# The last projection of a decoder block as Strassen's seven block products, its weight sums made on GpSimd during the attention

## The chip, the cores and the metric

One core of one Trainium2 chip runs the whole program. The metric is the device time of one execution in microseconds (us), the median of the runs shown. One more execution was profiled; every row below is from it.

## The reference, cut to what matters

One layer of a decoder block with 1024 positions and a model width of 1024, in float32. Two places of it matter here: the stick-breaking attention (eight heads), during which the change lets GpSimd work, and the last product, with w_down (2816 x 1024), which the change rearranges.

```python
def _stick_breaking(q, k, v):
    for nb in range(T // QBLK):
        ...
        z = jnp.einsum('bhqd,bhkd->bhqk', qb, kb).astype(jnp.float32) * scale
        log_rest = jnp.where(mask, jax.nn.log_sigmoid(-z), 0.0)
        after = lax.cumsum(log_rest, axis=3, reverse=True) - log_rest
        a = jnp.where(mask, jnp.exp(jax.nn.log_sigmoid(z) + after), 0.0)
        outs.append(jnp.einsum('bhqk,bhkd->bhqd', a.astype(vb.dtype), vb))
...
        up = u @ w_up[layer]
        up = lax.conv_general_dilated(up, ...) + conv_b[layer]
        gate, val = up[..., :D_FF], up[..., D_FF:]
        h = h + (jax.nn.silu(gate) * val) @ w_down[layer]
    return _rms_norm(h, final_norm_w)
```

## The kernel before, in words

The program goes through input projections, the stick-breaking attention, the sparse attention, the output projection, the up product (`up`) and the down product (`down`). Nearly all float32 products are made as three matmuls: each operand is split into a high half (a copy by ScalarE, L193) and a low half (the rest, a subtraction, L194), and high x high, high x low and low x high are added up in PSUM. The up product is already done by Strassen's scheme in Winograd's form, with the names P1 to P7 (L1454 to L1456).

**The stick-breaking attention** (`sb_attend`). The work is cut into 48 pieces, each of two query blocks with up to four key blocks. `sb_front` makes the logits of a query block on TensorE (L425, L426, L428), two sigmoids on ScalarE (L429, L430), a running product on VectorE (the scan, L436), and the product of the two on GpSimd (L439, tile `A`, 96 of them; L441 clears the part above the diagonal). `sb_turn` transposes the finished `A` on TensorE (L455), two pieces later (`SB_LAG = 2`), and `sb_back` multiplies it with the values (L475). Between them a second generator, `fill`, is advanced: the projections of the next head pair, whose weights are loaded on SyncE's queue (`wr`, L204) and split by ScalarE and GpSimd (`wl`, L194). Each engine and SyncE's queue runs its instructions strictly in an order fixed when the program is built; the builder places an instruction where its inputs are expected to be ready, so that an engine's order need not be the order of the source.

**The down product** (`down`). The 2816 rows of w_down are 22 row blocks of 128, the 1024 positions two chunks of 512. For each chunk `c`, each of the 22 row blocks and each of four position blocks and two column halves, three matmuls of 512 columns run (`mms`, L1588 to L1590): 2 x 22 x 8 x 3 = 1056. In a chunk the eight PSUM banks hold the eight sums. `load_w` loads a row block of the weights once and splits it (ScalarE and GpSimd, tiles `dh`, `dl`; the first eight have their place in `qn` and `mts`, which the up product has left); `load_act` loads the activations `act_d`, which the up product has written to DRAM, and splits them on ScalarE and VectorE (`ah`, `al`). At each chunk's start and end four row blocks are taken together (`GROUP`), so that rows of the output end one after another; their residual is added (L1624), the squares are summed, and `finish` scales and stores them.

Of the kernel before, what the change touches and what calls it, by code (L numbers as in the profile page):

```python
# [10 lines left out]
F32 = mybir.dt.float32  # L11
F32R = mybir.dt.float32r
# [68 lines left out]
class Kern:  # L81
# [479 lines left out]
                    nc.vector.memset(self.score[rows, i, cur + 1:16], NEG)  # L561


    def compress_in(self, kv, wp, vp):

        nc, a = self.nc, self.a
        w = self.load_cols(wp, a["w_in"], (C_KC, C_VC)[kv], bufs=3, rbufs=2, parts=2)
        for c in range(2):
            pm = self.ps("mm")
            yield from self.mm3_steps(pm, [w[k] + self.u(k, c) for k in range(KT)])  # L570
            src = self.tl(vp, [P, 512], "vt")
            nc.scalar.activation(src, pm, AF.Copy)
            nc.sync.dma_start(self.kct_d[kv][:, c * 512:c * 512 + 512], src)
            yield
# [493 lines left out]
    def run(self):  # L1068
# [15 lines left out]
        with self.pool("sbv", "right") as vp:  # L1084
            st_b, st_a = ExitStack(), ExitStack()
            stk = [None, st_b.enter_context(self.pool("stkb", "right"))]
            stk[0] = st_a.enter_context(self.pool("stka", "right"))
            ops = []
            with self.pool("xin") as xin:
                proj = self.sb_project(0, wp, stk[0], vp, ops, xin)  # L1090
                self.load_norm(xin, vp, mxs, proj, stk[1])
                for _ in proj:
                    pass
            with self.pool("sbw") as work:
                fill, due = iter(()), 0.0
                got = [ops, [], [], []]

                def start(p):
                    nonlocal fill
                    for _ in fill:  # L1100
                        pass
                    if p < 3:
                        fill = self.sb_project(p + 1, wp, stk[1 - p % 2], vp, got[p + 1])
                    else:
                        st_a.close()
                        fill = self.compress_keys(st_a.enter_context(self.pool("cin", "right")), wp, vp)
                    self.pace = PACE[p == 3]
                    return got[p]

                for _ in self.sb_attend(start, work, mxs):  # L1110
                    due += self.pace
                    while due >= 1.0:
                        due -= 1.0
                        next(fill, None)
                for _ in fill:
                    pass
            st_a.close()
            st_b.close()
# [148 lines left out]
    def mlp(self, mxs):  # L1267
# [125 lines left out]
        for _ in fill:  # L1393
            pass
        st_r.close()
        self.weights, self.acts = {}, {}
        self.up(p1)
        self.down(st_up)

# [58 lines left out]
    def up(self, p1):  # L1458
# [3 lines left out]
        for i in range(NF):  # L1462
# [34 lines left out]
            if last:  # L1497
                for _ in range(AHEAD):
                    self.prepare()
                self.load_w(0)  # L1500
                self.load_w(1)
            bb = self.ps(tags[1])
            self.product(bb, i, "P6", True)
            u2 = self.scratch()
# [3 lines left out]
            u3 = self.scratch()  # L1508
            nc.vector.tensor_add(u3, bc, u2)
            if last:  # L1510
                for j in range(GROUP):
                    if j > 1:
                        self.load_w(j)
                    self.load_act(j, 0)
            bd = self.ps(tags[3])
            self.product(bd, i, "P5", True)

# [14 lines left out]
            gate(1)  # L1532


    def load_w(self, i):

        homes = ((self.qn, 0), (self.qn, 4), (self.mts, 4), (self.mts, 0))
        if i < 2 * len(homes):
            if i in self.weights:
                return  # L1540
            t, lo = homes[i // 2]
            v = t[:, lo:lo + 4].rearrange("p a b t -> p (a b t)")[:, 2048 * (i % 2):2048 * (i % 2) + 2048]
            dh, dl = v[:, 0:T], v[:, T:2048]
        else:
            dh, dl = (self.tl(self.dp, [P, T], t, 5, F32R) for t in ("dh", "dl"))
        raw = self.tl(self.rawp, [P, KT, P], "wr", 4).rearrange("p k c -> p (k c)")
        self.nc.sync.dma_start(raw, self.a["w_down"][i * P:(i + 1) * P, :])
        self.split_w(raw, dh, dl)
        self.weights[i] = (dh, dl)

    def load_act(self, i, c):

        if c == 0 and i < GROUP:
            raw = self.scratch()
            ah, al = (t[:, i, :] for t in self.R["P7"])
        else:
            raw = self.tl(self.dp, [P, 512], "ar", 3)
            ah, al = (self.tl(self.dp, [P, 512], t, 7, F32R) for t in ("ah", "al"))
        self.nc.sync.dma_start(raw, self.act_d[i][:, c * 512:c * 512 + 512])
        self.split_w(raw, ah, al, self.nc.vector)  # L1560
        self.acts[i, c] = (ah, al)

    def down(self, st_up):
        nc, a = self.nc, self.a
        weights, acts = self.weights, self.acts
        rows = []

        def finish(tb, y, ss):
            r = self.rstd(ss, 1, 1.0 / DM, True)
            nc.scalar.activation(y[:, 0:512], y[:, 0:512], AF.Copy, scale=r[:, 0:1])  # L1570
            nc.vector.scalar_tensor_tensor(y[:, 512:DM], hs[tb][:, 512:DM], r[:, 0:1], self.fnw[:, 512:DM],
                                           op0=ALU.mult, op1=ALU.mult)
            for i in range(2):
                nc.sync.dma_start(a["out"][tb * P:(tb + 1) * P, i * 512:i * 512 + 512], y[:, i * 512:i * 512 + 512])

        hs = {}
        with ExitStack() as st_2:
            for c in range(2):
                banks = {}

                def mms(i, tb, hf):
                    if (tb, hf) not in banks:
                        banks[tb, hf] = self.ps(("o", "z", "z", "z", "mb", "tr", "tr", "ma")[2 * tb + hf])
                    pd = banks[tb, hf]
                    ah, al = acts[i, c]
                    dh, dl = weights[i]
                    s, cs = slice(tb * P, tb * P + P), slice(hf * 512, hf * 512 + 512)
                    nc.tensor.matmul(pd, ah[:, s], dh[:, cs], start=i == 0, stop=False)  # L1588
                    nc.tensor.matmul(pd, ah[:, s], dl[:, cs], start=False, stop=False)  # L1589
                    nc.tensor.matmul(pd, al[:, s], dh[:, cs], start=False, stop=i == NF - 1)  # L1590

                def blocks(first, last, alone):

                    for i in range(first, last):
                        if (i, c) not in acts:
                            self.load_w(i)
                            self.load_act(i, c)
                        if not alone:
                            continue
                        for tb in range(4):  # L1600
                            for hf in range(2):
                                mms(i, tb, hf)

                blocks(0, GROUP, False)
                for tb in range(4):
                    for hf in range(2):
                        for i in range(GROUP):
                            mms(i, tb, hf)
                if c == 0:
                    st_up.close()  # L1610
                    self.dp = self.rawp = st_2.enter_context(self.pool("dp"))
                    self.fnw = self.tl(self.dp, [P, DM], "fnw")
                    nc.sync.dma_start(self.fnw, a["final_norm_w"].rearrange("(o c) -> o c", o=1).to_broadcast([P, DM]))
                blocks(GROUP, NF - GROUP, True)
                blocks(NF - GROUP, NF, False)
                for tb in range(4):
                    row = 4 * c + tb
                    h = hs[row] = self.tl(self.dp, [P, DM], "h", 4)
                    nc.sync.dma_start(h, self.h_d[row])
                    for hf in range(2):  # L1620
                        for i in range(NF - GROUP, NF):
                            mms(i, tb, hf)
                        cs = slice(hf * 512, hf * 512 + 512)
                        nc.vector.tensor_add(h[:, cs], banks[tb, hf], h[:, cs])  # L1624
                    y = self.tl(self.dp, [P, DM], "y", 3)
                    nc.gpsimd.tensor_mul(y[:, 0:512], h[:, 0:512], self.fnw[:, 0:512])
                    ss = self.square_sums(self.tl(self.nt, [P, 512], "na", 2), [h[:, 0:512], h[:, 512:DM]])
                    rows.append((row, y, ss))
                    if len(rows) > 1:
                        finish(*rows.pop(0))  # L1630
            while rows:
                finish(*rows.pop(0))


_INS = ["x", "norm1_w", "w_in", "cmp_pos_k", "cmp_pos_v", "cmp_k_w1", "cmp_k_w2", "cmp_v_w1", "cmp_v_w2",
# [27 lines left out]
```

## Time and profile before

| what | value |
|---|---|
| time, median of 3 runs | 1492.44 us (1489.34 to 1494.07) |
| the profiled execution's own time | 1489.68 us |
| its span, first to last instruction | 1487.9 us |
| mean granted TensorE clock | 0.993 of 2.4 GHz |
| TensorE busy | 1432.7 us, 96% |
| VectorE, ScalarE, GpSimd busy | 979.3, 793.7, 761.4 us |
| stick-breaking attention | about 48 to 350 us |
| down product, first to last matmul | 1239.0 to 1480.7 us |

How to read it: the span is 1.8 us shorter than the execution's own time, and that time lies 2.8 us under the median of the runs. A matmul's record is longer than its share of TensorE, since matmuls overlap: a 128x512 one is recorded with 389 ns, while 421 of them start in 95 us. In the views below the names `PE`, `DVE`, `ACT`, `POOL` and `SP` are TensorE, VectorE, ScalarE, GpSimd and SyncE.

### The profile page before, as it was taken

The page shows a single profiled execution, that of the slowest core. Times are in us where ns is not written, and L with a number is a line of the kernel's source. Part 1 is how long each engine was busy: PE and PEld are TensorE (multiplying, and loading weights), DVE is VectorE, ACT ScalarE, POOL GpSimd, SP SyncE. Part 2 cuts the span into 40 slices and gives each one's busy share as a digit, 9 for nine tenths or more (in the row PEclk, how much of TensorE's full clock was granted, in tenths as well). Part 3 has the DMA queues.
Part 4 walks back from the last instruction along what each step waited for, and adds up shares of the span by engine and source line. Part 5 has one row for each costly group of instructions (what it writes and reads, how often), then busy time and mean ns, then how long its engine had stood idle before and what let it go on. Part 6 is the DMA issues. An engine that isn't in the chain of part 4 may idle for free. (4 is left out here: it accounts for less than half of the span.)

```text
span 1487.9 us, 21917 instructions
## 1 busy us (share of the span) xinstructions
PE 1432.7 (96%) x7619; PEld 1200.9 (81%) x7619; DVE 979.3 (66%) x2018; ACT 793.7 (53%) x1691; POOL 761.4 (51%) x727
## 2 busy tenths in 40 slices
PE   7999999999899999999998899999999999999998
PEld 5777777777788988998887778888888887888886
DVE  5587878775257899997438687777778775414112
ACT  6576676653368888887324444444444453324122
POOL 3355655562326667664132566666666664545043
PEclk9999999999999999999999999999999999999999
DMA  5200100325311010003340222222222233845321
GB/s 195 71 22 22 29 22 22 96 65 162 113 30 30 1 57 2 1 16 114 128 135 22 78 78 85 86 85 85 85 86 85 79 113 116 298 140 192 103 92 57
DMA packets 113354, 122.75 MB, mean 83 GB/s; under 512 B 6988, under 2 KB 84444, under 8 KB 112988
## 3 DMA queue, kind: packets, MB, share of 16 engines
q1 hardware_dynamic: 113244, 121.36, 25.4%
q8 instruction: 60, 0.98, 0.3%
q14 instruction: 50, 0.41, 0.1%
HBM read 96.58 MB, written 24.75 MB: 82 GB/s over the span
## 5 line engine op out<-in xcount | busy, mean ns | idle before, releaser
L194 POOL TENSOR_TENSOR gl<-mxs,gh 128x512 fp32r<-128x512 f32 x88 | 116.5, 1325 | 66.3 <-ACT gh L193 63.0
L439 POOL TENSOR_TENSOR A<-A,tt 128x384 f32<-128x384 f32 (+3 forms) x96 | 95.8, 1002 | 97.1 <-DVE tt L436 50.5
L194 POOL TENSOR_TENSOR gl<-wr,gh 128x512 fp32r<-128x512 f32 x66 | 85.7, 1301 | 103.2 <-ACT gh L193 80.5
L194 DVE TENSOR_TENSOR al<-ar,ah 128x512 fp32r<-128x512 f32 x40 | 42.1, 1063 | 128.6 <-ACT ah L193 110.4
L194 POOL TENSOR_TENSOR dl<-wr,dh 128x1024 fp32r<-128x1024 f32 x28 | 69.7, 2495 | 102.8 <-ACT dh L193 90.7
L186 DVE TENSOR_TENSOR pl<-ps_tr,ph 128x512 fp32r<-128x512 f32 (+1 forms) x175 | 111.9, 642 | 13.1 <-ACT ph L185 11.6
L185 ACT ACTIVATE ph<-ps_tr 128x512 fp32r<-128x512 f32 (+1 forms) x175 | 98.0, 563 | 42.0 <-PE ps_tr L455 24.8
L193 ACT ACTIVATE gh<-mxs 128x512 fp32r<-128x512 f32 x88 | 55.3, 629 | 65.3 <-PE ps_ma L1455 22.1
L436 DVE TENSOR_TENSOR_SCAN tt<-tt 128x384 f32<-128x384 f32 (+1 forms) x64 | 69.8, 1093 | 28.3 <-ACT tt L429 27.8
L194 POOL TENSOR_TENSOR wl<-wr,wh 128x512 fp32r<-128x512 f32 x40 | 54.9, 1377 | 62.2 <-ACT wh L193 60.4
L193 ACT ACTIVATE ah<-ar 128x512 fp32r<-128x512 f32 x40 | 25.0, 628 | 110.2 <-PE ps_ma L1589 101.5
L429 ACT ACTIVATE tt<-ps_z 128x384 f32<-128x384 f32 (+3 forms) x96 | 47.6, 496 | 43.0 <-PE ps_z L428 20.2
L734 POOL TENSOR_SCALAR lgw<-lgw,r,gates 128x640 f32<-128x640 f32 (+4 forms) x64 | 48.2, 764 | 36.4 <-DVE r L732 15.7
L193 ACT ACTIVATE gh<-wr 128x512 fp32r<-128x512 f32 x66 | 40.9, 623 | 43.3 <-DMA wr<-w_up_d 15.1
L219 PE MATMUL ps_ma<-uh,wh 128*128 128x512 f32 x136 | 60.4, 444 | 1.2 <-ACT wh L193 1.2
L220 PE MATMUL ps_ma<-ul,wh 128*128 128x512 f32 x136 | 55.2, 406 | 2.1 <-DVE ul L189 2.1
L221 PE MATMUL ps_ma<-uh,wl 128*128 128x512 f32 x136 | 55.2, 406 | 0.6 <-POOL wl L194 0.6
L455 PE MATMUL ps_tr<-ident,A 128*128 128x128 f32 x320 | 49.1, 277 | 6.4 <-DVE pl L186 2.6
L455 PEld LDWEIGHTS ps_tr<-ident,A 128*128 128x128 f32 x320 | 37.1, 142 | 16.0 <-DVE osb L501 3.2
L1483 ACT ACTIVATE na<-na 128x512 f32<-128x512 f32 x44 | 27.6, 628 | 39.9 <-DVE na L1479 39.9
L1434 DVE TENSOR_TENSOR mxs<-mxs,wr 128x512 f32<-128x512 f32 x22 | 35.3, 1604 | 19.8 <-POOL mxs L1433 19.7
L430 ACT ACTIVATE A<-ps_z 128x384 f32<-128x384 f32 (+3 forms) x96 | 47.4, 493 | 0.1
(683 smaller groups left out, 5193.5 us busy)
## 6 DMA issues: line engine op xcount, KB each, us to landing
wr<-w_up_d SPq DMA_DIRECT2D x44, 512.0 KB, 5.0
wr<-w_down_d SPq DMA_DIRECT2D x36, 512.0 KB, 4.7
act_d<-na SPq DMA_DIRECT2D x44, 256.0 KB, 3.9
wr<-w_in_d SPq DMA_DIRECT2D x40, 256.0 KB, 2.8
ar<-act_d SPq DMA_DIRECT2D x40, 256.0 KB, 2.5
h<-h_d SPq DMA_DIRECT2D x8, 512.0 KB, 4.7
out_d<-y SPq DMA_DIRECT2D x16, 256.0 KB, 2.2
mxs<-x_d SPq DMA_DIRECT2D x4, 512.0 KB, 3.5
```

Of the source, the lines that this page charges most:

```text
L185: nc.scalar.activation(hi, src, AF.Copy)
L186: nc.vector.tensor_sub(lo, src, f(hi))
L193: nc.scalar.activation(hi, raw, AF.Copy)
L194: (eng or nc.gpsimd).tensor_sub(lo, raw, f(hi))
L219: nc.tensor.matmul(out, lh, rh, start=(i == 0), stop=False)
L220: nc.tensor.matmul(out, lh, rl, start=False, stop=False)
L221: nc.tensor.matmul(out, ll, rh, start=False, stop=(i == last))
L429: nc.scalar.activation(tt[:, 0:w], z[:, :w], AF.Sigmoid, scale=-1.0)
L436: nc.vector.tensor_tensor_scan(rev, rev, rev, 1.0 if carry[j] is None else carry[j], op0=ALU.mult, op1=ALU.bypass)
L439: nc.gpsimd.tensor_mul(A[:, j, 0:w], A[:, j, 0:w], tt[:, 1:w + 1])
L455: nc.tensor.transpose(pt[:, kk * 256 + j * P:kk * 256 + (j + 1) * P], A[:, j, c0:c0 + P], self.ident)
L734: nc.gpsimd.tensor_scalar(lg[i][:, :L], lg[i][:, :L], r[:, i:i + 1], gate[:, i:i + 1], op0=ALU.mult, op1=ALU.mult)
```

## The change: seven block products, and sums made beforehand

The change has two parts. **In `down`** the activations (1024 x 2816) and w_down (2816 x 1024) are each taken as 2 x 2 blocks, `a11` to `a22` and b11 to b22, and the product is formed in seven block products (`DOWN`), each over 11 row blocks: `fetch` loads the pieces, `halves` makes the activations' sums on VectorE and splits both operands on ScalarE and VectorE, and `mms` runs three matmuls for each of four position blocks. 7 x 11 x 4 x 3 = 924 matmuls take the place of 1056. There are 77 rounds of 12 matmuls; loads are called for six rounds ahead of the matmuls and halves four rounds ahead; the split operands lie in eight places of `qn` and `mts`. Two sets of four PSUM banks are used in turn, and `evacuate` adds a product's banks to what is kept.

**In the stick-breaking attention** a generator `down_sums` makes the four sums of w_down's blocks that four of the products need, and writes them to DRAM (`td`). It takes 44 pieces (11 row blocks times four column quarters): two loads of 128x2x128 into one of three tiles `ts`, four subtractions of 128x128 on GpSimd in that tile, one store of the tile. It is advanced once for each step of `sb_attend`.

```diff
+    def down_sums(self, pool):
+        nc, n = self.nc, NF // 2
+        src = self.a["w_down"].rearrange("(b i p) (h q c) -> b i q p h c", b=2, p=P, h=2, q=4)
+        self.td = [self.dram.tile([P, 4, 512], F32, name=f"td{j}") for j in range(n)]
+        places = [(j, q) for j in range(n) for q in range(4)]
+        tiles = {}
+        for r in range(len(places) + 2):
+            if r < len(places):
+                j, q = places[r]
+                t = tiles[r] = self.tl(pool, [P, 4, P], "ts", 3)
+                for b in range(2):
+                    nc.sync.dma_start(t[:, 2 * b:2 * b + 2, :], src[b, j, q])
+            yield
+            if r < 2:
+                continue
+            j, q = places[r - 2]
+            t = tiles.pop(r - 2)
+            b11, b12, b21, b22 = (t[:, i, :] for i in range(4))
+            for out, x, y in ((b22, b12, b22), (b12, b12, b11), (b11, b11, b22), (b21, b21, b11)):
+                nc.gpsimd.tensor_sub(out, x, y)
+                yield
+            yield
+            nc.sync.dma_start(self.td[j][:, :, P * q:P * q + P], t)
+            yield
...
+                sums = self.down_sums(work)
                 for _ in self.sb_attend(start, work, mxs):
+                    next(sums, None)
...
+                for _ in sums:
+                    pass
...
+    ND = NF // 2
+    DOWN = ("P1", "P6", "P2", "P7", "P5", "P4", "P3")
...
+        if name == "P1":
+            v = act(0, 0, self.scratch() if n < GROUP else keep("a11"))
+        elif name == "P6":
+            v = act(0, 1, passing())
+            act(1, 1, keep("a22"))
+            if j < GROUP:
+                act(0, 0, keep("a11"))
+        elif name in ("P2", "P3"):
+            v = act(1, 0, passing())
+        w = self.scratch()
...
+        if name == "P6":
+            s2 = kept["s2", j] = self.tl(self.dp, [P, 512], "s2", self.ND)
+            nc.vector.tensor_add(s2, v, kept["a22", j])
+            nc.vector.tensor_sub(s2, s2, kept["a11", j])
+            v = s2
+        elif name == "P7":
...
+            nc.vector.tensor_sub(v, kept["s2", j], kept["a22", j])
...
+        self.split_w(v, ah, al, nc.vector)
+        self.split_w(w, bh, bl, nc.vector)
...
+            while fetched < min(n + 7, 7 * ND):
+                self.fetch(fetched)
+                fetched += 1
+            while made < min(n + 5, 7 * ND):
+                self.halves(made)
+                made += 1
```

**Where the instructions stand now.** On GpSimd, at the start of the attention, the order before is this (`A` are the attention's products, `wl` the low halves of projection weights):

```order
L441 MEMSET A_606 128x128
L194 TENSOR_TENSOR wl_642<-wr_640,wh_641 128x512
L194 TENSOR_TENSOR wl_919<-wr_917,wh_918 128x512
L441 MEMSET A_646 128x128
L439 TENSOR_TENSOR A_606<-A_606,tt_607 128x128
L439 TENSOR_TENSOR A_606<-A_606,tt_618 128x256
L441 MEMSET A_672 128x128
L439 TENSOR_TENSOR A_646<-A_646,tt_647 128x384
L439 TENSOR_TENSOR A_646<-A_646,tt_662 128x512
L439 TENSOR_TENSOR A_672<-A_672,tt_673 128x384
```

and now, with the new subtractions `ts`:

```order
L441 MEMSET A_606 128x128
L584 TENSOR_TENSOR ts_629<-ts_629 128x128 x4
L584 TENSOR_TENSOR ts_642<-ts_642 128x128 x4
L584 TENSOR_TENSOR ts_675<-ts_675 128x128 x4
L194 TENSOR_TENSOR wl_659<-wr_657,wh_658 128x512
L584 TENSOR_TENSOR ts_760<-ts_760 128x128 x4
L584 TENSOR_TENSOR ts_849<-ts_849 128x128 x4
L584 TENSOR_TENSOR ts_927<-ts_927 128x128 x3
L194 TENSOR_TENSOR wl_966<-wr_964,wh_965 128x512
...
L439 TENSOR_TENSOR A_663<-A_663,tt_682 128x512
L584 TENSOR_TENSOR ts_1013<-ts_1013 128x128 x2
L439 TENSOR_TENSOR A_693<-A_693,tt_694 128x384
```

The rest of GpSimd's order in the attention, and TensorE's, VectorE's and ScalarE's orders there, are as they were. Of the 176 subtractions 24 stand ahead of the first product `A`, the next 150 between it and the 38th product, and the last two just behind that one; from the 39th to the 96th product there is none.

On SyncE's queue the loads (L576) and stores (L588) of the sums in the same stretch, among the loads `wr`:

```order
L576 DMA ts_629<-w_down_d 128x2x128 x2
L576 DMA ts_642<-w_down_d 128x2x128 x2
L576 DMA ts_675<-w_down_d 128x2x128 x2
L588 DMA td_618<-ts_629 512x1x128
L588 DMA td_618<-ts_642 512x1x128
L588 DMA td_618<-ts_675 512x1x128
L576 DMA ts_760<-w_down_d 128x2x128 x2
L576 DMA ts_849<-w_down_d 128x2x128 x2
L576 DMA ts_927<-w_down_d 128x2x128 x2
L204 DMA wr_970<-w_in_d 128x4x128
L588 DMA td_618<-ts_760 512x1x128
```

Three tiles go round: a tile's next load stands behind the store of what it held three pieces earlier, and a store waits for the tile's four subtractions.

On VectorE, in the rounds of P6 of the down product (L1611 and L1612 make the activations' sum, L194 the low halves, which lie in `qn` and `mts`):

```order
L1611 TENSOR_TENSOR s_14062<-ar_14006,a_14008 128x512
L194 TENSOR_TENSOR qn<-s_14036,qn 128x512
L1612 TENSOR_TENSOR s_14062<-s_14062,a_14010 128x512
L194 TENSOR_TENSOR mts<-mxs,mts 128x512
L1611 TENSOR_TENSOR s_14086<-ar_14029,a_14031 128x512
L194 TENSOR_TENSOR mts<-s_14062,mts 128x512
L1612 TENSOR_TENSOR s_14086<-s_14086,a_14033 128x512
```

A round of P6 has four such operations on VectorE; a round of P7, P5 and P3 has three, one of P1, P2 and P4 two. GpSimd, which made the weights' low halves before, has none of them now.

## Rows read from the trace of the kernel before

**Rows 1.** The page's part 1: busy time of each engine.

```profile
PE 1432.7 (96%) x7619; PEld 1200.9 (81%) x7619; DVE 979.3 (66%) x2018; ACT 793.7 (53%) x1691; POOL 761.4 (51%) x727
```

**Rows 2.** Engine busy time by stretch: attention's start, to the 38th product, rest; down product.

```profile
core 0: us, PE busy (x) PEld busy (x) DVE busy (x) ACT busy (x) POOL busy (x), PEclk, DMA share, GB/s
48.00:66.40 18.40, 18.00 (x87) 14.52 (x86) 5.12 (x13) 7.73 (x16) 3.69 (x5) 1.00 0.20 57
66.40:167.50 101.10, 96.64 (x561) 78.31 (x560) 80.67 (x142) 69.45 (x150) 59.76 (x66) 1.00 0.10 24
167.50:350.00 182.50, 175.74 (x1031) 143.96 (x1030) 134.83 (x230) 114.40 (x243) 106.12 (x117) 0.99 0.17 45
1239.00:1481.00 242.00, 239.84 (x1057) 197.99 (x1055) 68.99 (x84) 74.59 (x115) 95.42 (x54) 1.00 0.43 150
1365.00:1460.00 95.00, 95.00 (x421) 78.69 (x420) 16.50 (x18) 20.61 (x28) 30.71 (x15) 1.00 0.29 99
```

**Rows 3.** Timeline of TensorE in the down product: its one wait.

```profile
1263.25 0.50 PE L1590 MATMUL ps_o<-mts,al 128*128 128x512 f32 x1 [1.88 <-DVE al L194]
```

**Rows 4.** Operations of the down product by tile: ns min/median/max, first and last start.

```profile
L194 DVE TENSOR_TENSOR al<-ar,ah x40: 675/694/2896, 1260.8 to 1443.1; 128x512 fp32r<-128x512 f32 x40
L194 POOL TENSOR_TENSOR dl<-wr,dh x28: 2393/2397/2962, 1268.5 to 1454.7; 128x1024 fp32r<-128x1024 f32 x28
```

**Rows 5.** The page's part 5: the same VectorE operation with its mean.

```profile
L194 DVE TENSOR_TENSOR al<-ar,ah 128x512 fp32r<-128x512 f32 x40 | 42.1, 1063 | 128.6 <-ACT ah L193 110.4
```

**Rows 6.** Timeline of GpSimd in the attention: start, us, operation, idle before.

```profile
111.48 0.20 POOL L169 TENSOR_SCALAR rv<-hss 128x8 f32<-128x8 f32 x1 [0.21 <-DVE hss L318]
111.76 1.66 POOL L170 TENSOR_TENSOR ry<-rv,mhalf 128x8 f32<-128x8 f32 x1
113.50 1.05 POOL L322 TENSOR_TENSOR mxs<-osb,ry 128x512 f32<-128x512 f32 x1
...
131.13 0.41 POOL L439 TENSOR_TENSOR A<-A,tt 128x128 f32<-128x128 f32 x1 [0.28 <-DVE tt L436]
...
145.83 1.09 POOL L439 TENSOR_TENSOR A<-A,tt 128x512 f32<-128x512 f32 x1 [2.28 <-ACT tt L484]
...
173.05 1.09 POOL L439 TENSOR_TENSOR A<-A,tt 128x512 f32<-128x512 f32 x1 [1.53 <-DVE tt L436]
```

**Rows 7.** Timeline of TensorE: transposes of the two products that end GpSimd's rows above.

```profile
148.44 0.60 PE L455 MATMUL ps_tr<-ident,A 128*128 128x128 f32 x4
...
174.05 0.61 PE L455 MATMUL ps_tr<-ident,A 128*128 128x128 f32 x4
```

**Rows 8.** Waits in the attention, 48 to 350 us: total, times, longest.

```profile
POOL A L439 <- DVE tt L436: 50.5, 35, 3.2
```

**Rows 9.** DMA issues: KB each, median us from issue to landing; stretch 66.4 to 167.5.

```profile
q1 hardware_dynamic: 4722, 2.34, 9.4%
...
wr<-w_in_d SPq DMA_DIRECT2D x8, 256.0 KB, 2.8
```

**Rows 10.** DMA issues: stores over the whole span, and SyncE's time for an issue.

```profile
act_d<-na SPq DMA_DIRECT2D x44, 256.0 KB, 3.9
...
h_d<-h SPq DMA_DIRECT2D x8, 256.0 KB, 2.0
...
L204 SPq DMA_DIRECT2D wr<-w_in_d x33: 367/368/506, 4.3 to 320.5; - x33
```

**Rows 11.** TensorE by stretch, with the granted clock, late in the attention.

```profile
320.00:323.00 3.00, 1.67 (x11) 0.99 0.66 202
323.00:326.40 3.40, 3.40 (x11) 0.50 0.17 43
```

## Prediction: the seven products against the sums on GpSimd

> **What bounds the kernel now.** I read the page's busy times first [rows 1]: TensorE is busy for 96% of the span, the others for 51 to 66%. So time is won where TensorE has less to do, and lost where it has to wait. Then the busy times by stretch [rows 2], for the two places that the change touches.
>
> In the down product TensorE is full and nothing else is: in the steady part 421 matmuls start in 95.00 us, 0.2257 us each, while VectorE is busy for 16.5 us of it and GpSimd for 30.7 [rows 2]. Its one wait is 1.88 us, at the fifth row block [rows 3]. There a matmul less is 0.2257 us less.
>
> In the attention TensorE is busy for 114.6 of 119.5 us up to the 38th product `A` (18.00 + 96.64 [rows 2]), but it hangs on GpSimd closely. Two products of 1.09 us end at 146.92 and 174.14 [rows 6]; the transposes that read them start at 148.44 and at about 174.1 [rows 7], 1.5 us and none later. GpSimd itself is busy for 59.76 of 101.10 us there [rows 2]; its idle time is mostly spent on VectorE's scan (50.5 us over the whole attention [rows 8]). So GpSimd has 41.3 us to give in this stretch, and what it takes beyond that comes out of TensorE's time, since TensorE can't make up lost time at 96%.
>
> **The down product.** Removed: 1056 - 924 = 132 matmuls x 0.2257 us = **-29.8 us**. That holds if the rounds of 12 matmuls (2.71 us) are fed.
> - VectorE. 77 rounds x 2 low halves + 55 sums of activations (P6 22; P7, P5, P3 11 each) = 209 operations, and 24 for the banks, of 0.69 us [rows 4]: 161 us in the 924 x 0.2257 = 208.5 us. A round of P6 has four, 2.78 us against 2.71; with halves four rounds ahead, 11 x 0.07 us is hidden. The price of 0.69 is the median; the mean was 1.063 [rows 5], as the same operation stretches to 2.9 us [rows 4] while GpSimd makes `dl` beside it. Those 2.4 us operations [rows 4] go, so I take 0.69. Cost 0; if that cover is gone, see the third rival.
> - ScalarE splits the same number of elements as now or fewer; at 74.6 of 242 us busy [rows 2] it has room.
> - Loads. P6 needs three pieces of 256 KB in a round of 2.71 us, 290 GB/s, for 11 rounds, where the stage now moves 150 GB/s at a share of 0.43 [rows 2], so at most some 350. With six rounds' lead I cost it at 0.
> - Start. Only 48 matmuls (10.8 us) cover the loads and splits of the fifth round, in place of 96 (21.7 us). The present wait of 1.88 us may go, stay, or grow: -1.9 to +3, taken as 0. The additional low halves beside the last up block (8 x 0.69 us on VectorE, four more than now) are hidden there or cost up to 2 us; taken as 0.
> - The end has the same chain per row (add, squares, scale, store), with 12 matmuls (2.7 us) between the last rows in place of 24: 0 to +1.
>
> Together -29.8 us, between -32 and -24.
>
> **The sums on GpSimd.** They are not spread over the whole attention: in the order as built 24 of the 176 stand ahead of the first product, 150 before the 38th. So the stretch from 66.40 to 167.50 us gets all of these 150.
>
> What does one cost? The product of 128x128 has the same form, two inputs and in place: 0.41 us [rows 6]. But the four of a piece build on one another and each waits for the one before. The nearest rows are L169, L170 and L322, which do the same: the next starts 0.08 us after the end (111.68 to 111.76, 113.42 to 113.50 [rows 6]). So one is 0.41 us at least and 0.49 where it waits. I take 0.49, as three of four wait.
>
> Work of GpSimd in the stretch: 59.76 + 150 x 0.49 = 133.3 us for 101.1: **+32.2 us**. With 0.41: 121.3, +20.2 us. The 24 ahead take 24 x 0.49 = 11.8 us of the 14.7 us in which GpSimd is idle between 48 and 66.4 us [rows 2], but come in two sets of three tiles with a load and a store between, so that the first product comes some 2 us late: +2. TensorE's margin to the products, up to 1.5 us, takes about 2 away with the waits that it has now: -2.
>
> The three tiles. A tile goes through a load, four subtractions, a store, and only then the next load. With 2.8 us for a load of 256 KB in pieces of 512 bytes [rows 9], 4 x 0.49, a store of 2.0 to 3.9 us and 0.37 us for each of three issues [rows 10] that is 7.9 to 9.8 us, or 2.6 to 3.3 us for a piece; GpSimd's own pace would be 133.3 / 37.5 = 3.55. So the ring alone does not bound, but where several pieces stand together without a product between them, GpSimd waits for a load with products queued behind it, and TensorE behind these. The engines of the DMAs are near their limit too: 44 x 512 KB = 23.1 MB, where 2.34 MB took 9.4% of 101 us [rows 9], so about 246 GB/s in such pieces: 94 us of all engines. Between 0 and the second rival's figure I take **+5**, nearer to 0, as the two paces leave room. The 132 issues are 132 x 0.37 = 49 us on SyncE's queue; the `wr` loads behind the stores come later with them, but so do their users. GpSimd stops making the weights' halves in `down`, which saves nothing on any path.
>
> Sum: -29.8 + 32.2 + 2 - 2 + 5 = **+7.4 us**. From the profiled execution's 1489.7 that is 1497.1; that execution lies 2.8 us under the median of the runs (1492.4), so on the scale of the median about **1500**.
>
> The price of the matmuls can be read otherwise. The Trainium skill, page "TensorE: Matmul & The Clock Gate", section "Back-to-back issue gap", gives about 131 ns for a 512-column matmul in a sustained stream; by it the 132 would give back only 17.3 us and the sum would be +19.9. The trace's 226 ns for this stage decides here.
>
> **The rivals.**
> 1. *The sums fit into GpSimd's idle time* (the other side: faster). The 41.3 us of idle hold 150 sums of up to 0.275 us. The part of an operation that grows with its columns is (1.09 - 0.41) / 3 = 0.23 us for 128 columns [rows 6]; if short operations in a row overlap their fixed part, 150 x 0.23 = 34 us fits, and only some 2 us of jitter stay: 1489.7 - 29.8 + 2 = 1461.9, about 1465 on the median's scale. For it: GpSimd waits in small pieces now [rows 8] that a short operation fills. Against it: 0.08 us between dependent operations, the opposite of an overlap. The decisive point is 0.275 us a sum. The Trainium skill, page "GPSIMD Engine Reference", section "Elementwise — side-by-side cycle accounting", measures 4497 ns for 2048 elements of a two-input operation; an estimate from that page is 281 ns for 128 without a fixed part, which would just about fit. The trace's 0.41 us speaks against it. Chance 0.20.
> 2. *The ring of three tiles bounds.* Loads and stores queue on each other in SyncE's strict order and at the DMA engines: a load of 4.0 (2.8 and a blocked issue), 2.0 of sums, a store of 3.9, 1.1 of issues and 1.8 for a product or two ahead in GpSimd's order are 12.8 us for three pieces, 4.27 each, 160 us for the 37.5: +59 in place of +37.2. 1489.7 - 29.8 + 59 = 1518.9, about 1522. Chance 0.17.
> 3. *VectorE becomes the bound of the down product.* If its operations keep the mean of 1.063 us [rows 5], the 233 take 247.7 us for 208.5: +39, which leaves about 1539. It decides from 208.5 / 233 = 0.89 us each. Against it: GpSimd has some 20 operations left there. Chance 0.06.
>
> **How the numbers follow.** My forecast has 0.57. Its own range: the sums between +20 and +45, the down product between -32 and -24, so 1480 to 1513 on the median's scale. A measurement of this kernel can tell 0.3%, 4.5 us, from no change: 1488 to 1497. The forecast's part below that is 0.07, within 0.17, above 0.33. With the rivals: faster 0.20 + 0.07 = 0.27, the same 0.17, slower 0.33 + 0.17 + 0.06 = 0.56. The range reaches from 1470 (the larger part of the first rival lies below it, some 0.13) to 1526 (the third rival, 0.06, lies above): 0.81 inside.
>
> Within it I have one thing that I can't price: TensorE's clock. Late in the attention it was busy for 1.67 of 3 us, and in the next 3.4 us the granted clock was 0.50, 1.2 GHz [rows 11]. If waits in the stretch bring TensorE that low, some 3.4 us parts run at half the pace; GpSimd is the slower one there anyway, so I add nothing, and the upper end stands for it.
>
> **What would show it right or wrong.** In the changed profile: the down product's matmuls 924 at 0.226 us, ending about 209 us after they start, VectorE's `L194` there at 0.69 us; a 128x128 subtraction with 0.41 us and 0.08 us between; GpSimd busy for over 90% from the first to the 38th product, and that stretch 30 to 45 us longer; TensorE's transposes (L455) and their weight loads waiting for `A`. Wrong is the forecast if the stretch grows by less than 20 us, or if GpSimd is found idle before subtractions that wait for a load for more than some 15 us in all (then the ring is the bound), or if the down product's matmuls are spaced by VectorE.

## The result, and the profile after

The changed kernel takes 1516.84 us in the median (1512.78 to 1518.47); the kernel before, in the same runs, 1490.89. The ratio is 1.0167, with a 95% interval of 1.0139 to 1.0195: 26 us slower, where +7.4 was forecast. The profiled execution of the changed kernel took 1512.8 us (span 1510.7), 4 us under its median, so its trace explains 22.8 us of span.

The page's part 1 of the changed kernel, as [rows 1]:

```profile
PE 1417.4 (94%) x7487; PEld 1185.5 (78%) x7487; DVE 1074.3 (71%) x2191; ACT 820.2 (54%) x1769; POOL 780.2 (52%) x879
```

The same stretches as [rows 2]: from the first to the 38th product `A`; the down product; its steady part:

```profile
core 0: us, PE busy (x) PEld busy (x) DVE busy (x) ACT busy (x) POOL busy (x), PEclk, DMA share, GB/s
73.84:226.21 152.37, 115.00 (x583) 90.63 (x583) 82.78 (x141) 71.22 (x151) 135.61 (x218) 0.90 0.51 147
1293.00:1502.00 209.00, 209.00 (x923) 172.74 (x921) 163.79 (x248) 100.40 (x189) 34.46 (x31) 1.00 0.55 189
1350.00:1445.00 95.00, 95.00 (x421) 78.68 (x420) 80.15 (x112) 40.23 (x71) 18.56 (x12) 1.00 0.48 165
```

The down product does what was said of it. The 924 matmuls start at 1292.4 and end at 1502.0, with the pitch of before (421 in 95 us) and no wait; the 1.88 us of [rows 3] are gone. 209.6 us take the place of 241.7 (1239.0 to 1480.7), and the end behind the last matmul is 1.5 us longer (8.7 for 7.2): -30.6.

The attention loses 53.4 us: the down product starts that much later (at 1292.4 for 1239.0). The stretch of 101 us up to the 38th product has become 152.4. GpSimd's groups in it:

```profile
line engine op names shapes xcount | busy us, mean ns | idle before us <-releasers
L584 POOL TENSOR_TENSOR ts<-ts 128x128 f32<-128x128 f32 x151 | 81.3, 542 | 16.2 <-DMA ts<-w_down_d 8.1 <-issue 0.8
L439 POOL TENSOR_TENSOR A<-A,tt 128x512 f32<-128x512 f32 x15 | 18.2, 1215 | 0.0
L194 POOL TENSOR_TENSOR wl<-wr,wh 128x512 fp32r<-128x512 f32 x8 | 10.8, 1356 | 0.0
```

and what it waits for there, the whole list:

```profile
engine line waited for: us in total, times, longest us
POOL ts L584 <- DMA ts<-w_down_d: 8.1, 8, 2.1
POOL ts L584 <- issue: 0.8, 2, 0.6
POOL rv L169 <- DVE hss L318: 0.2, 1, 0.2
```

GpSimd no longer waits for a product's inputs: "idle before" a product is 0.0. Before the change, between the first and the 38th product, it had waited for VectorE's scan alone for 17.2 us (50.5 us in the whole attention [rows 8]):

```profile
POOL A L439 <- DVE tt L436: 17.2, 11, 3.0
```

TensorE now waits for GpSimd. Its transposes of `A` have 42.0 us of idle time before them in the whole run, where they had 6.4 (the releaser named is only the one that came last). Before the change and after it:

```profile
L455 PE MATMUL ps_tr<-ident,A 128*128 128x128 f32 x320 | 49.1, 277 | 6.4 <-DVE pl L186 2.6
L455 PE MATMUL ps_tr<-ident,A 128*128 128x128 f32 x320 | 53.5, 290 | 42.0 <-DVE pl L186 16.2
```

TensorE's granted clock in the stretch is 0.90 of 2.4 GHz in the mean: 30.7 of the 152.4 us were at 1.2 GHz. As the list above has no wait of GpSimd for TensorE, I take it that this clock adds nothing to the stretch; no run shows it by itself. The timeline of GpSimd shows the pattern, with subtractions between the products:

```profile
93.79 2.88 POOL L584 TENSOR_TENSOR ts<-ts 128x128 f32<-128x128 f32 x4
96.63 1.09 POOL L439 TENSOR_TENSOR A<-A,tt 128x512 f32<-128x512 f32 x1
97.68 0.99 POOL L584 TENSOR_TENSOR ts<-ts 128x128 f32<-128x128 f32 x2
98.63 1.29 POOL L194 TENSOR_TENSOR wl<-wr,wh 128x512 fp32r<-128x512 f32 x1
99.88 1.42 POOL L584 TENSOR_TENSOR ts<-ts 128x128 f32<-128x128 f32 x3
```

The second price is the wait for a load with a product queued behind it. Here are the scan that makes the 24th product's input, the subtractions before that product, and the product:

```profile
146.95 1.95 DVE L436 TENSOR_TENSOR_SCAN tt<-tt,tt 128x512 f32<-128x512 f32 x1 [0.18 <-ACT tt L429]
155.99 2.06 POOL L584 TENSOR_TENSOR ts<-ts 128x128 f32<-128x128 f32 x4 [0.93 <-DMA ts<-w_down_d]
158.00 1.30 POOL L439 TENSOR_TENSOR A<-A,tt 128x512 f32<-128x512 f32 x1
```

The input is there at 148.90, and the product starts 9.1 us later. From the end of its scan and sigmoid to its start, one of the first 38 products now stands in GpSimd's queue for 5.9 us in the mean; before the change it was 0.5 us.

### The profile page after: what moved, and what is told of

Read it like the earlier page. It is cut to its first block, busy times and chain, and to the rows that moved or that the text cites. A ratio compares the mean times of both kernels' runs of the same rounds, so it can differ in the third digit from the quotient of the medians.

```text
span 1510.7 us, 22537 instructions
## 1 busy us (share of the span) xinstructions
PE 1417.4 (94%) x7487; PEld 1185.5 (78%) x7487; DVE 1074.3 (71%) x2191; ACT 820.2 (54%) x1769; POOL 780.2 (52%) x879
## 5 line engine op out<-in xcount | busy, mean ns | idle before, releaser
L194 POOL TENSOR_TENSOR gl<-mxs,gh 128x512 fp32r<-128x512 f32 x88 | 116.9, 1330 | 68.9 <-ACT gh L193 65.6
L194 POOL TENSOR_TENSOR gl<-wr,gh 128x512 fp32r<-128x512 f32 x66 | 85.7, 1300 | 103.3 <-ACT gh L193 76.4
L186 DVE TENSOR_TENSOR pl<-ps_tr,ph 128x512 fp32r<-128x512 f32 (+1 forms) x175 | 111.9, 642 | 15.4 <-ACT ph L185 11.3
L584 POOL TENSOR_TENSOR ts<-ts 128x128 f32<-128x128 f32 x176 | 94.3, 540 | 22.7 <-DMA ts<-w_down_d 13.2
L436 DVE TENSOR_TENSOR_SCAN tt<-tt 128x384 f32<-128x384 f32 (+1 forms) x64 | 70.3, 1100 | 37.4 <-ACT tt L429 22.2
L455 PE MATMUL ps_tr<-ident,A 128*128 128x128 f32 x320 | 53.5, 290 | 42.0 <-DVE pl L186 16.2
L193 ACT ACTIVATE gh<-mxs 128x512 fp32r<-128x512 f32 x88 | 55.3, 629 | 65.1 <-PE ps_z L1487 21.2
L1692 POOL TENSOR_TENSOR a<-a,p 128x512 f32<-128x512 f32 x8 | 12.6, 1580 | 139.1 <-DMA a<-h_d 125.7
L194 POOL TENSOR_TENSOR wl<-wr,wh 128x512 fp32r<-128x512 f32 x40 | 54.3, 1363 | 46.6 <-ACT wh L193 44.3
L219 PE MATMUL ps_ma<-uh,wh 128*128 128x512 f32 x136 | 63.5, 467 | 1.5 <-ACT wh L193 1.5
L436 DVE TENSOR_TENSOR_SCAN tt<-tt,tt 128x256 f32<-128x256 f32 (+1 forms) x32 | 39.5, 1236 | 14.9 <-issue 7.5
L219 PE MATMUL ps_mb<-late,wh 128*128 128x512 f32 x112 | 47.4, 424 | 0.0
```

Source lines behind the costliest of these rows:

```text
L186: nc.vector.tensor_sub(lo, src, f(hi))
L193: nc.scalar.activation(hi, raw, AF.Copy)
L194: (eng or nc.gpsimd).tensor_sub(lo, raw, f(hi))
L219: nc.tensor.matmul(out, lh, rh, start=(i == 0), stop=False)
L436: nc.vector.tensor_tensor_scan(rev, rev, rev, 1.0 if carry[j] is None else carry[j], op0=ALU.mult, op1=ALU.bypass)
L455: nc.tensor.transpose(pt[:, kk * 256 + j * P:kk * 256 + (j + 1) * P], A[:, j, c0:c0 + P], self.ident)
```

## The experiments

Theory A says that GpSimd's own time is the main cost. Theory B says that it is the ring of three tiles with its loads, stores and traffic. Theory C says that any subtraction delays the products by its share, whatever is idle. The change and twelve kernels, with the medians of their runs:

| kernel | us | above the one without subtractions |
|---|---|---|
| the change | 1516.8 | 55.3 |
| no subtractions | 1461.5 | 0 |
| four tiles | 1524.7 | 63.2 |
| spread over the attention | 1487.8 | 26.3 |
| wide, one tile | 1497.8 | 36.2 |
| half of the subtractions | 1495.3 | 33.7 |
| pairs, four tiles | 1522.3 | 60.8 |
| in `up` | 1523.2 | 61.7 |
| in `up`, wide | 1490.9 | 29.4 |
| resident tiles | 1499.8 | 38.3 |
| resident tiles, half | 1469.1 | 7.6 |
| wide, spread | 1473.6 | 12.1 |
| in `up`, wide, spread | **1467.1** | 5.5 |

The kernel before took 1490.9 us beside the change and 1493.2 to 1494.1 beside the twelve, so a difference between rows can be off by some 3 us. Four rows leave out work that the result needs and tell of times only: no subtractions, half of them, and the two with resident tiles.

**No subtractions.**

```diff
-            for out, x, y in ((b22, b12, b22), (b12, b12, b11), (b11, b11, b22), (b21, b21, b11)):
-                nc.gpsimd.tensor_sub(out, x, y)
+            for _ in range(4):
                 yield
```

> Leaves out the 176 subtractions: td then holds the blocks of w_down themselves, not their sums; the loads, the stores and the seven products stay. Theory A (GpSimd's work is the whole cost): the attention is as long as before the change within 3 us, and the total is 1516.8 - 54 = about 1463 (1458 to 1468). Theory B (the three tiles, their loads and stores, and the DMA traffic bound the stretch): the transfers alone keep 15 us or more of the 54, so 1475 or above. In both the down product ends 209 to 211 us after it begins.

Measured 1461.5, ratio to the kernel before 0.9781 (0.9757 to 0.9805). The whole loss hangs on the subtractions: the stretch is what it was, though the DMA engines move 221 GB/s at a share of 0.77 in it (before 24 GB/s at 0.10, [rows 2]):

```profile
66.73:167.81 101.08, 96.57 (x561) 78.31 (x560) 80.62 (x142) 69.36 (x150) 59.82 (x66) 1.00 0.77 221
```

So the traffic alone costs nothing in this stretch. The run also gives the down product's own worth: 1494.1 - 1461.5 = 32.6 us against the kernel before in the same runs, 29.4 us against its 1490.9 beside the change. In the traces it is 30.6 us.

**The subtractions without their loads.** Three tiles are loaded once, nothing is stored, the down product reads blocks of w_down, and the subtractions stay between the same products.

```diff
+        tiles = [self.tl(pool, [P, 4, P], f"ts{r}") for r in range(3)]
...
+        for r in range(4 * 11):
+            t = tiles[r % 3]
...
+            if self.muls < len(self.BEHIND):
+                with self.tc.issue_after(mul.ins):
+                    self.some_sums(self.BEHIND[self.muls])
```

> The 176 subtractions stand where they stand in the changed kernel, between the same products, but work again and again on three tiles loaded once: the other 41 pieces' loads and all stores are left out, and the down product reads blocks of w_down in place of the sums. Theory A (GpSimd's time is the main cost, the waits for loads the smaller one): the stretch grows by 81 us of subtractions + 7 us of waits between them - 41 us of idle time = 47 us less what the loads' waits took, so 1461.5 + 42 to 48 = 1503 to 1510. Theory B (the ring with its loads is the main cost, and GpSimd's time fits): below 1480.

Measured 1499.8, 4 us less than theory A's lower bound and far above theory B's 1480. GpSimd's time by itself is 38.3 us of the 55.3. From the first to the 38th product it is busy for 137.8 of 141.7 us, with the DMA engines at a share of 0.08:

```profile
69.20:210.90 141.70, 110.86 (x580) 87.81 (x581) 82.41 (x142) 71.11 (x152) 137.79 (x218) 0.92 0.08 19
```

The other 17.0 us went with what this kernel leaves out: 13.2 us of waits for loads in the changed kernel from 48 us on (this one has 5.9, for its first load), and some 5 us of short waits of one subtraction for another (28 of some 0.08 us in the stretch, 91 in the change). I take it that there are fewer of these because pieces on two tiles take turns; the rows do not name the tile, so that is not shown. Theory B is out as the main cause and stays as the second.

**Half of the subtractions**, with all transfers, and on resident tiles. (Left out are the sums for P6 and P4; the first text names the wrong pair.)

```diff
-            for out, x, y in ((b22, b12, b22), (b12, b12, b11), (b11, b11, b22), (b21, b21, b11)):
+            for out, x, y in ((b22, b12, b22), (b12, b12, b11)):
                 nc.gpsimd.tensor_sub(out, x, y)
+                yield
                 yield
```

> Leaves out two of the four subtractions of each piece (the ones that make the sums for P5 and P7), 88 in place of 176; all transfers stay. Theory A (a capacity: only what exceeds GpSimd's idle time of 41 us in the stretch is paid): 75 x about 0.58 = 43 us ahead of the 38th product, so almost nothing above the kernel without subtractions (1461.5): 1463 to 1476. Theory C (each subtraction delays the products behind it by its own share, idle time or not): half of the 55 us, 1486 to 1492.

> The same with two of the four subtractions of each piece: 88 on resident tiles. The kernel with half the subtractions and all the transfers took 1495 us, with 26 us of waits for loads on GpSimd. Theory A with the ring as the second bound: without the loads 76 x 0.56 = 43 us meet 41 us of idle time, so 1463 to 1476. Theory C (each subtraction delays the products by a share of its time, whatever is idle): 1485 or above.

Measured 1495.3 and 1469.1. The first is a miss of theory A, and lies above even theory C's 1492. The second tells why: without loads 88 subtractions cost 7.6 us, as theory A has it, so most of the room is there. The stretch is 110.0 us for 101.0:

```profile
67.90:177.90 110.00, 101.16 (x573) 81.30 (x572) 83.23 (x143) 70.98 (x154) 102.50 (x143) 0.98 0.09 22
```

With loads the ring bounds. GpSimd's waits in the two, in the attention:

```profile
POOL ts L584 <- DMA ts<-w_down_d: 24.5, 14, 5.9
POOL ts L584 <- issue: 11.6, 6, 3.8
```

```profile
POOL ts L582 <- DMA ts<-w_down_d: 4.3, 1, 4.3
```

Half the work was paid for with waits: 24.5 + 11.6 us in place of 13.2 + 0.8. Of the 24.5 us 9.8 stand ahead of the first product, which comes at 69.1 us, 2.4 us later than without subtractions; between the first and the 38th product it is 14.7 + 11.6 in place of 8.1 + 0.8. For the 11.6 us the profile names no cause; the longest, 3.8 us up to 165.35, follows loads that were issued from 161.54 on. On SyncE's queue the stores wait 28.4 us for subtractions in the stretch, and the loads stand behind them. So the two bounds lie one behind the other: with fewer subtractions the loads set the pace.

**Four tiles, and pairs.** The first only adds a tile and loads a piece earlier; the second also holds the subtractions of two pieces in turn.

```diff
-                t = tiles[r] = self.tl(pool, [P, 4, P], "ts", 3)
+                t = tiles[r] = self.tl(pool, [P, 4, P], "ts", 4)
...
+            for o, x, y in ((3, 1, 3), (1, 1, 0), (0, 0, 3), (2, 2, 0)):
+                for t in pair:
+                    with self.tc.issue_after(last) if last is not None else ExitStack():
+                        last = nc.gpsimd.tensor_sub(t[:, o, :], t[:, x, :], t[:, y, :]).ins
```

> Four tiles in the ring in place of three, the loads one piece further ahead. Theory A: GpSimd waited for a load for 13 us in all, and the order puts the sums even denser, so 1505 to 1520. Theory B: a ring of four turns in the same time with a third more pieces, which takes a quarter off the sums' stretch: at least 15 us less, 1502 or below.

> Four tiles, and the subtractions of two pieces in turn, held in that order, so that none waits for the one before it. To be compared with the four tiles alone (1524.7). Theory A: a subtraction then takes 0.41 to 0.42 us from start to start in place of 0.54 in three of four, 0.12 x 0.75 x 150 = 13.5 us less ahead of the 38th product: 1508 to 1515. Rival: the wait is no loss of GpSimd's (the recorded 0.46 us stays, and VectorE's scans, not the chain, make a subtraction long): 1520 to 1528.

Measured 1524.7 and 1522.3. The first misses both theories. With four tiles the builder placed the subtractions denser still (173 before the 30th product, 140 in the change), and waits for loads were not fewer (15.0 us). The second misses theory A and lies where its rival has it, and the 2.4 us between the two are within the spread of their runs. But the rival's reason isn't borne out either: in turn, no subtraction waits for the one before, and one takes 0.51 us of the stretch up to the start of what follows (77.8 us for 152) in place of 0.57 (84.8 for 148), so that wait is a real price. The waits for loads then rise from 15.0 to 25.6 us and take the gain.

**Spread, and wide.** The same work held back in the order; then 11 pieces of 512 columns in one tile; then both.

```diff
+            self.last_mul = nc.gpsimd.tensor_mul(A[:, j, 0:w], A[:, j, 0:w], tt[:, 1:w + 1]).ins
...
+                with self.tc.issue_after(self.last_mul):
+                    nc.gpsimd.tensor_sub(out, x, y)
```

> The same subtractions, each held in GpSimd's order behind the attention's product that stands before it in the source, so that 60 rather than 174 of them stand ahead of the 38th product and the rest go on to the end of the attention. Theory A: over the whole attention GpSimd has 132 us of idle time (14.7 + 41.3 + 76.4) for 176 x 0.6 = 106 us, so most of the loss goes: 1465 to 1490. Theory C (each sum ahead of a product delays TensorE by its own time wherever it stands, since TensorE is full): as the change, 1510 to 1525. Theory B has the same ring with half the pace, and would lose its cost too.

> 11 pieces of 512 columns in one tile in place of 44 of 128 columns in three: the same sums in 44 operations. Theory A: 44 x (1.09 + 0.08) = 51 us of GpSimd in place of about 106, 35 of them (41 us) ahead of the 38th product, which is what it has idle there: 1465 to 1482. Theory B: one tile means load, sums and store one after another, 11 x some 13 to 15 us with products queued behind subtractions that wait for a load: 1505 or above.

> 11 pieces of 512 columns in one tile, 44 subtractions, each held behind the product that stands before it in the source, so that they spread over the whole attention and a load has seven steps' time to land. Theory A with the ring: 44 x 1.4 = 62 us in 132 us of idle time, no wait for a load, some 1 us of delay where a product stands behind a subtraction: 1465 to 1478. Theory C: as the wide pieces without the hold, 1490 to 1498.

Spread: 1487.8, as theory A has it, near its upper end. GpSimd is busy for 264 of 297 us from the first to the last product, so little room is left. Wide in one tile: 1497.8, between the two theories and a miss of both; the one tile brings 28.1 us of waits for loads, and a subtraction takes 1.46 us, not 1.09. Both together: 1473.6, ratio 0.9861 (0.9829 to 0.9893). GpSimd in the attention with the wide pieces, without and with the hold:

```profile
L577 POOL TENSOR_TENSOR ts<-ts 128x512 f32<-128x512 f32 x44 | 64.3, 1462 | 29.7 <-DMA ts<-w_down_d 28.1
```

```profile
L578 POOL TENSOR_TENSOR ts<-ts 128x512 f32<-128x512 f32 x44 | 67.0, 1523 | 0.1
```

The same work and 24 us less: the waits are gone, and nothing stands in a dense block. The edit has two parts, the hold and seven steps in place of four between a load and its subtractions; no run parts them here.

**In the up product.** The same pieces moved; then wide in two tiles; then each held behind a weights' low half. (The advance shown is that of the wide ones; the narrow ones advance two or three steps at a time.)

```diff
+        for _ in range(1 if i < NF - 2 else 99):
+            next(getattr(self, "dsums", iter(())), None)
...
+                with self.tc.issue_after(self.last_low):
+                    nc.gpsimd.tensor_sub(out, x, y)
```

> The same 44 pieces, loads, subtractions and stores, advanced in the up product in place of the attention. GpSimd is busy for 62% there, and what it makes (weights' halves) is made some products ahead. Theory A: the attention is as before the change; the up product takes the 176 x 0.6 = 106 us into about 140 us of idle time with buffers between: 1462 to 1475. Theory C (TensorE is full in the up product too, so each subtraction delays it): 1490 or above.

> As the one before, with 11 pieces of 512 columns in two tiles: 44 subtractions. Theory A: 44 x 1.3 to 1.5 us = 57 to 66 us of GpSimd, less than half of its idle time: 1460 to 1468, and not above the 44 narrow pieces. Theory C: 1475 or above.

> The 11 wide pieces in the up product, each subtraction held behind the weights' low half that stands before it in the source, about one for every three products of the up stage. Theory A with the ring: GpSimd goes from 62% to about 80% with no dense part and no wait for a load: 1461 to 1470. Theory C (any subtraction beside a full TensorE delays it): as without the hold, 1485 to 1493.

Measured 1523.2, 1490.9 and 1467.1. The first two miss theory A and lie where theory C has them. But the builder again packs the subtractions together. The narrow ones stand between 840 and 1035 us; from 850 to 1100 us GpSimd is busy for 195.9 of 250 us and waits 23.9 us for loads, while TensorE is busy for 206:

```profile
850.00:1100.00 250.00, 206.02 (x812) 162.67 (x811) 149.50 (x225) 87.84 (x162) 195.85 (x253) 0.92 0.51 152
```

The wide ones without the hold stand between 846 and 975 us, with 3.7 us of waits for loads. Held, they stand between 840 and 1196 us and cost 5.5 us. In 900 to 1200 us, without the hold and with it:

```profile
900.00:1200.00 300.00, 286.35 (x1227) 235.01 (x1226) 222.65 (x303) 130.03 (x233) 212.29 (x162) 0.97 0.37 121
```

```profile
900.00:1200.00 300.00, 296.32 (x1302) 243.68 (x1301) 225.51 (x323) 133.12 (x246) 230.93 (x173) 1.00 0.41 138
```

The hold is the only difference between these two. More work on GpSimd and TensorE full: theory C falls here, as it does with the subtractions spread (1487.8) and with half of them on resident tiles (1469.1). This kernel is faster than both, with a ratio of 0.9822 (0.9787 to 0.9856) to the kernel before.

## Why the prediction was wrong in size

The sign and the place were right: the down product's term came as said, and GpSimd overflows between the first and the 38th product. The time lies in the range, but the forecast's +7.4 is 26 (22.8 in the profiled executions). Two prices were too small, by about as much each: that of a sum on GpSimd, and that of the loads. By the steps of the sum:

1. *132 matmuls, -29.8*: -30.6 in the traces, and -29 to -33 by the run without subtractions. The other terms taken as 0 there hold: VectorE's low halves have a median of 0.69 us, and no round waits.
2. *150 sums at 0.49 us, +32.2*: this step failed. They are 150 subtractions of 0.54 us in the mean, with 91 waits of 0.08 us between dependent ones (7.1 us in all). The stretch's account: 81.4 us of subtractions, 58.8 of GpSimd's other work, 7.1 of short waits and 9.2 of longer ones, less 4.6 of overlap between neighbours, with 0.5 of rest, is 152.4. Work and short waits make 142.7, +41.7 us above the 101.0 of before: 9.5 more than forecast.
3. *+5 for waits on loads*: 9.2 us of waits over 0.15 us in the stretch, 8.1 of them for loads and 0.8 without a cause in the profile.
4. *+2 at the first product*: it comes 7.4 us late (66.5 to 73.8); 5.1 us of waits for loads stand ahead of it. Steps 3 and 4 together are 16.6 us for 7, again 9.6 more than forecast. The reason given, that the paces of ring and GpSimd leave room, failed too: with half the subtractions the ring still took 134.7 us for 38 pieces, 3.5 us each, where 2.6 to 3.3 had been worked out with all four subtractions. I placed the ring as a rival to GpSimd's time; the runs show both in one sum. The second rival's time, 1522, is nearer than the forecast, but that is luck: its mechanism isn't the main one (38.3 us against 17.0).
5. *-2 for TensorE's margin*: 58.7 us at the 38th product are 53.4 at the down product, so some 5 us are made up on the way; where, no run shows.

Added up as measured: -30.6 + 41.7 + 9.6 (the longer waits and the rest) + 7.4 - 5.3 = 22.8 us.

Of the signs named, GpSimd's share came out just under 90% (135.6 of 152.4 us), the stretch grew by 51 us, not 30 to 45, and the waits for loads stayed just under 15 us (13.2).

The first rival fell: its decisive point was 0.275 us a sum, against 0.54. The third fell with VectorE at 0.69 us.

Where does 0.54 come from? The first part is that the price was a product's, 0.41 us, and a subtraction takes longer: its median is 0.459 us. The trace of before shows it with 512 columns, where a product takes 1.09 us [rows 6] and a low half, which is a subtraction, 1.30:

```profile
L194 POOL TENSOR_TENSOR gl<-wr,gh 128x512 fp32r<-128x512 f32 x66 | 85.7, 1301 | 103.2 <-ACT gh L193 80.5
```

The second part is a few long ones. Of the 176 subtractions 27 last over 0.6 us, 26.5 us together, and during 18.2 us of these VectorE runs its scan (L436), which lies beside 23 of the 27; the other 149 take 68.5 us, with the scan beside 7.1 us. VectorE's `pl` (L186), which reads PSUM and one SBUF tile, lies beside both kinds alike (4.1 and 9.1 us). One such pair, GpSimd and VectorE:

```profile
87.45 1.41 POOL L584 TENSOR_TENSOR ts<-ts 128x128 f32<-128x128 f32 x1
```

```profile
87.66 0.94 DVE L436 TENSOR_TENSOR_SCAN tt<-tt 128x384 f32<-128x384 f32 x1
```

The subtraction ends 0.26 us after the scan. The Trainium skill, page "SBUF — State Buffer", section "Who interferes with whom", says that a VectorE instruction with two inputs in SBUF contends with a GpSimd instruction that reads SBUF, and that one with at most one SBUF input does not, outside VectorE's 2-port modes. The trace agrees with both halves, as far as overlaps can show it. The nearest run is the one with the narrow pieces in the up product, where no scan runs: 16 of its 176 subtractions last over 0.6 us, 13.8 us together, and the mean is 0.50. So the scan is not the only neighbour that goes with long subtractions, and its share isn't shown by a run of its own. The prediction's estimate of 281 ns for 128 columns, from the Trainium skill, page "GPSIMD Engine Reference", section "Elementwise — side-by-side cycle accounting", had no fixed part; the trace's median is 459 ns.

## What to carry to other kernels

Idle time of an engine with a strict order is room only for work that is ready when its turn comes: price both the added time, from rows of the same operation and at its mean beside the neighbour that it collides with, and the waits that it brings into the queue. Work that a source spreads evenly can stand in a dense block as built; read the order, and hold each piece behind an instruction where there is room. Fewer, wider operations, held apart, in a stage whose engine works ahead of TensorE made 5.5 us out of 55.3.

## What was not expected of the hardware

The DMA engines at a share of 0.77 and 221 GB/s cost no time from the first to the 38th product (101.1 us with them, 101.0 before). A 128x512 product on GpSimd took 1.09 us [rows 6], and a subtraction of the same size 1.29 us in the median and 1.46 to 1.52 in the mean in the attention; one of 128x128 took up to 1.44 us. Halving GpSimd's subtractions there, with their transfers kept, gave back 21.6 us of 55.3; on resident tiles, 30.7 of 38.3.
